# Byte addresses of SBUF tiles modulo 128, and three ones-products on TensorE, in a two-layer decoder trunk

## Chip, cores and metric

One NeuronCore of one Trainium2 chip. The metric is the device time of one execution in microseconds (us); lower is better.

## What is computed

Two layers of a decoder trunk on 256 tokens of width 1024, in float32. Each layer normalises the rows of x, scales and shifts them by a conditioning vector, mixes tokens with 8 stick-breaking and 8 sparse-attention heads, and then applies a channel mixer: a SwiGLU network of width 2816 in layer 0, the two best of eight experts of width 3584 in layer 1. Cut to what matters here:

```python
for layer in range(2):
    mod = silu(c) @ w_ada[layer] + b_ada[layer]        # six vectors of 1024
    h = rms_norm(x, g_pre_mix) * (1 + scale_m) + shift_m
    proj = h @ w_in                                    # q, k, v of all heads, gates
    merged = concat(rms_norm(o_sb, g_sb), rms_norm(o_nsa, g_nsa))
    x = x + gate_m * rms_norm(merged @ w_out, g_post_mix)
    h = rms_norm(x, g_pre_ffn) * (1 + scale_f) + shift_f
    f = swiglu(h) if layer == 0 else moe(h)            # router: h @ w_router + b_router, top 2 of 8
    x = x + gate_f * rms_norm(f, g_post_ffn)
```

## The kernel before

The work goes through five stages: layer 0's mixer (with a start that brings in x and the first weights), the dense channel mixer (`ffn`), layer 1's mixer, then routing and the eight experts (`moe`). Weights stream in by DMA, 1 MB a transfer, from the SP queue into the tiles `raw` (a ring of six) and, in the experts, also `unit`.

**Products.** Most of the matrix work runs in split form. A weight half-tile of 128x1024 is split by ScalarE (`whi`, L179) and VectorE (`wlo`, L180) into two parts of type float32r, the rows likewise (`hh` and `hlo` by `norm_parts` and `first`, `on` and `os` in the mixers, `gh`/`gl` and `xgh`/`xgl`/`g` in the channel mixers), and `mm3` (L193 to L197) makes three matmuls of them. A matmul has a stationary operand (128 columns, loaded ahead of it) and a moving operand that is streamed past. In two shapes the moving operand has:

- **256 columns**: the input projections and `ffn_gate`/`ffn_up`. Mostly `hh` or `hlo` moves past `whi`/`wlo` (`proj_t`, `ffn`); in `proj` (v of each head) the weights move past `hh`/`hlo`. `ffn` has 11 units of 96 such matmuls, each mixer some 530.
- **512 columns**: the output projection `wo`, `ffn_down` (into `acc`) and the large experts. The weights move past `on`/`os`, `gh`/`gl`, `xgh`/`xgl` or `g`. There are 96 in each `wo`, 264 in `ffn_down`, and 4 large experts with 504 each.

Four of the experts are small (64 slots): they use plain float32 and `unit`/`raw` themselves move (L1041).

**Addresses.** A tile pool puts tiles one behind another. The tile `sm` (L92) has 248 floats, or 992 bytes, `brow` (L122) 32 bytes, so that everything behind them starts off a multiple of 128 bytes. In the built program the start addresses modulo 128 are, with what each is used as in `mm3`:

| tiles | layer 0's mixer | ffn | layer 1's mixer | experts |
|---|---|---|---|---|
| `raw`, `unit`, `whi`, `wlo` | 64 | 64 | 64 | 64 |
| `hh`, `hlo` | 0 | 64 | 64 | |
| `on`, `os` | 0 | | 64 | |
| `gh`, `gl`; `xgh`, `xgl`, `g` | | 64 | | 64 |

So a 256-column matmul has its two operands at remainders 0 and 64 in layer 0 and at 64 and 64 in `ffn` and layer 1; a 512-column one 64 and 0 in layer 0's `wo`, and 64 and 64 everywhere else.

**Three small products with ones.** The squares of the mixers' outputs are summed over channels on TensorE: `sparse` (L706 to L709) multiplies the four 128x128 quarters of `sq` by a column of ones, in each of two row blocks t; `stick` (L758 to L763) keeps four tiles `sqs`, one for each pair of heads, and does eight such products at its end. `level` (L826 to L836) multiplies eight columns of the shift with eight slices of the router's weights and adds the bias. Each float32 matmul here shows as two instructions in the profile.

**Order.** A scheduler places the instructions of each engine by estimated times; an engine then runs its own list strictly in order.

Of the kernel before, what the change touches and what calls it, by code (L numbers as in the profile page):

```python
# [15 lines left out]
OP = mybir.AluOpType  # L16
AX = mybir.AxisListType
# [43 lines left out]
class Kernel:  # L61
# [28 lines left out]
    def setup(self, st):  # L90
        tc, nc, const = self.tc, self.nc, self.const
        self.sm = const.tile([P, SM_N], F32, name="sm")  # L92
        nc.sync.dma_start(self.sm, self.ins["sm"])
        self.sc = self.mix.tile([P, SC_N], F32, name="sc")
# [26 lines left out]
        nc.vector.tensor_scalar(self.tie, self.tie, 0.0, None, op0=OP.is_lt)  # L121
        self.brow = const.tile([P, E], F32, name="brow")  # L122
        nc.sync.dma_start(self.brow, self.ins["moe_b"].to_broadcast([P, E]))
# [171 lines left out]
    def norm_parts(self, l, ph, gain, scale_i, shift_i):  # L295

        nc = self.nc
        ss, sh = self.affine(l, gain, scale_i), self.mod(l, shift_i)
        xn = self.rows(ph)
        hh, hl = (ph.tile([P, KT, S], F32R, name=n, tag="h8") for n in ("hh", "hlo"))  # L300
        for t in range(2):
            for h in range(2):
                p = self.bank("ps"[h], "xnT").rearrange("p (k t) -> p k t", k=4)
                hf = ph.tile([P, 4, P], F32, name="hf", tag="t2")
                for i in range(4):
                    k = 4 * h + i
# [11 lines left out]
        return hh, hl  # L318

    def first(self, ph):  # L320


        nc = self.nc
        oh = ph.tile([33, W], F32, name="oh", tag="t2")
        nc.sync.dma_start(oh, self.ins["onehot"])
        tab = ph.tile([33, 8], F32, name="tab")
        nc.vector.memset(tab, BIG)
# [7 lines left out]
        xn = self.rows(ph)  # L335
        hh, hl = (ph.tile([P, KT, S], F32R, name=n, tag="h8") for n in ("hh", "hlo"))
        banks = [self.bank("ssoopp"[i], "first").rearrange("p (m t) -> p m t", m=2) for i in range(6)]
# [10 lines left out]
        for q in range(4):  # L348
# [65 lines left out]
    def mixer(self, l, ph):  # L414
        nc = self.nc
# [83 lines left out]
        kcT, vc = self.compress(l, ph, cb)  # L499
        on = ph.tile([P, 2, 4, S], F32R, name="on", tag="h8")  # L500
        ssn = self.sparse(l, ph, qn, ks, vs, kcT, vc, gt, on)
# [42 lines left out]

        os_ = ph.tile([P, 2, 4, S], F32R, name="os", tag="h8")
        pairs = self.stick(l, ph, qT, kT, vv, os_)
        next(pairs)
        next(pairs)
        if l:
            level = self.level(l)  # L550
        wout(1, on, ssn, first)
# [54 lines left out]
    def sparse(self, l, ph, qn, ks, vs, kcT, vc, gt, out):  # L606


        nc = self.nc
        ssn = ph.tile([P, 2], F32, name="ssn")  # L610
        for t in range(2):
# [213 lines left out]

    def level(self, l):  # L826
# [40 lines left out]
    def route(self, ph, gt, eq):  # L867
# [551 lines left out]
```

## Time and profile before

| | |
|---|---|
| median of 3 runs | 1452.79 us (1452.57 to 1456.24) |
| the profiled execution | 1452.78 us, span of its instructions 1451.0 us |
| TensorE busy | 1379.9 us, 95% of the span, 7470 matmuls |
| VectorE, ScalarE busy | 977.9 us (67%), 770.0 us (53%) |
| HBM read | 479.87 MB, 332 GB/s over the span |

A matmul's busy time in this profile includes the way through the array, so that matmuls overlap and a busy TensorE is not TensorE at its peak. The pace of a run of matmuls is read from their start times: last start less first start, over the number of steps between them.

### The profile page before, as it was taken

Reading aid. Unit: us, or ns where it says so; the run is one execution under the profiler, and the core shown is the slowest. Engines: PE = TensorE matmul, PEld = TensorE weight load, DVE = VectorE, ACT = ScalarE, POOL = GpSimd, SP = SyncE. Lnnn points to the kernel's source line nnn. Section 1 sums busy time; section 2 is a strip of 40 time slices with the busy share of each in tenths; the row PEclk is TensorE's granted clock in tenths of the full one; section 3 lists DMA queues with packets and bytes.
Section 4 is the critical chain, followed back from the end, with each engine's and each line's share of the span. In section 5 each row is a group of like instructions: output and inputs, shape, how many; then the busy total and the mean of one; then the engine's idle time right before and its main releaser. Section 6 shows DMA issues by size and latency. Waiting matters only on the chain.

```text
span 1451.0 us, 20370 instructions
## 1 busy us (share of the span) xinstructions
PE 1379.9 (95%) x7470; PEld 988.8 (68%) x7470; DVE 977.9 (67%) x1566; ACT 770.0 (53%) x1179; POOL 16.5 (1%) x24
## 2 busy tenths in 40 slices
PE   5899969999979999999999999999999999999996
PEld 5767759999877687544788534887435888788432
DVE  7678888877565774522999424998315989999413
ACT  3464654444554556232787324787324778787322
POOL 0100010000100000000000000000000000000000
PEclk9989979999979999799999999999999999999998
DMA  9936829888435284899999999999999999999994
GB/s 365 326 143 210 337 82 344 316 309 315 176 119 203 88 319 132 353 400 420 419 421 420 419 419 420 420 420 421 418 421 420 420 420 407 345 368 375 369 421 182
DMA packets 73479, 482.52 MB, mean 333 GB/s; under 512 B 10315, under 2 KB 10484, under 8 KB 18588
## 3 DMA queue, kind: packets, MB, share of 16 engines
q1 hardware_dynamic: 72876, 479.91, 83.7%
q0 software_dynamic: 496, 1.25, 0.4%
q8 instruction: 60, 0.98, 0.3%
q14 instruction: 47, 0.39, 0.1%
HBM read 479.87 MB, written 1.25 MB: 332 GB/s over the span
## 4 chain that ended last, share of the span: by engine, by line
PE 64%; DVE 3%; ACT 1%; issue 1%; DVEq 0%; ACTq 0%
PE moe_gate L1041 7%; PE moe_up L1041 7%; PE yacc L1041 7%; PE moe_gate L196 4%; PE moe_gate L195 4%; PE moe_gate L197 4%; PE yacc L196 3%; PE yacc L195 3%; PE yacc L197 3%; PE moe_up L196 3%; PE moe_up L197 3%; PE moe_up L195 3%; PE gT L1099 2%; PE gather L1177 1%; DVE wlo L180 1%; PE po L618 1%
## 5 line engine op out<-in xcount | busy, mean ns | idle before, releaser
L179 ACT ACTIVATE whi<-raw 128x1024 fp32r<-128x1024 f32 x260 | 271.7, 1058 | 162.6 <-PE ffn_gate L196 33.0
L180 DVE TENSOR_TENSOR wlo<-raw,whi 128x1024 fp32r<-128x1024 f32 x256 | 307.0, 1223 | 74.1 <-ACT whi L179 68.8
L180 DVE TENSOR_TENSOR wlo<-unit,whi 128x1024 fp32r<-128x1024 f32 x202 | 236.7, 1221 | 9.3 <-ACT whi L179 5.4
L179 ACT ACTIVATE whi<-unit 128x1024 fp32r<-128x1024 f32 x202 | 208.4, 1057 | 34.0 <-PE moe_up L197 16.1
L207 DVE CUSTOM_DVE_ANT_0 raw<-raw,cb,sm 128x1024 f32<-128x1024 f32 x96 | 120.7, 1279 | 3.1 <-DMA raw<-in_w_ada_dram 3.1
L1089 DVE TENSOR_TENSOR sg<-moe_gate,sg 64x512 f32<-64x512 f32 x28 | 19.1, 681 | 113.5 <-ACT sg L1088 113.5
L196 PE MATMUL moe_up<-wlo,xgh 128*128 128x512 f32 x224 | 88.6, 395 | 3.9 <-DVE wlo L180 3.9
L196 PE MATMUL yacc<-wlo,g 128*128 128x512 f32 x224 | 89.3, 399 | 0.3 <-DVE wlo L180 0.3
L195 PE MATMUL moe_gate<-whi,xgh 128*128 128x512 f32 x224 | 88.2, 394 | 0.0
L195 PE MATMUL yacc<-whi,g 128*128 128x512 f32 x224 | 88.0, 393 | 0.0
L196 PE MATMUL moe_gate<-wlo,xgh 128*128 128x512 f32 x224 | 87.9, 392 | 0.0
L195 PE MATMUL moe_up<-whi,xgh 128*128 128x512 f32 x224 | 87.7, 392 | 0.0
L197 PE MATMUL yacc<-whi,g 128*128 128x512 f32 x224 | 87.4, 390 | 0.0
L197 PE MATMUL moe_up<-whi,xgl 128*128 128x512 f32 x224 | 87.4, 390 | 0.0
L197 PE MATMUL moe_gate<-whi,xgl 128*128 128x512 f32 x224 | 87.4, 390 | 0.0
L1089 DVE TENSOR_TENSOR up<-moe_up,up 64x512 f32<-64x512 f32 x28 | 19.1, 683 | 72.7 <-ACT up L1088 72.7
L1041 PE MATMUL moe_up<-unit,xf 128*64 128x512 f32 x288 | 66.3, 596 | 0.0
L1041 PE MATMUL yacc<-unit,gf 128*64 128x512 f32 x272 | 62.2, 593 | 0.0
L1041 PE MATMUL moe_gate<-unit,xf 128*64 128x512 f32 x240 | 57.1, 598 | 0.0
L1088 ACT ACTIVATE sg<-moe_gate 64x512 f32<-64x512 f32 x28 | 16.6, 594 | 72.6 <-PE moe_gate L1041 72.6
L195 PE MATMUL ffn_gate<-hh,whi 128*128 128x256 f32 x176 | 51.2, 291 | 2.5 <-ACT hh L315 2.4
L196 PEld LDWEIGHTS moe_up<-wlo,xgh 128*128 128x128 f32 x224 | 42.0, 188 | 16.6 <-DVE wlo L180 8.2
(410 smaller groups left out, 2926.1 us busy)
## 6 DMA issues: line engine op xcount, KB each, us to landing
unit<-in_moe_gate_dram SPq DMA_DIRECT2D x66, 1024.0 KB, 14.9
unit<-in_moe_up_dram SPq DMA_DIRECT2D x56, 1024.0 KB, 14.6
unit<-in_moe_down_dram SPq DMA_DIRECT2D x54, 1024.0 KB, 16.1
raw<-in_w_ada_dram SPq DMA_DIRECT2D x48, 1024.0 KB, 6.5
raw<-in_moe_gate_dram SPq DMA_DIRECT2D x46, 1024.0 KB, 14.5
raw<-in_moe_down_dram SPq DMA_DIRECT2D x45, 1024.0 KB, 15.6
raw<-in_moe_up_dram SPq DMA_DIRECT2D x44, 1024.0 KB, 13.7
raw<-in_w_in_dram SPq DMA_DIRECT2D x16, 1024.0 KB, 5.8
```

The source lines that it names most:

```text
L179: self.last_hi = nc.scalar.activation(hi, w, AF.Copy)
L180: last_lo = (nc.gpsimd if self.count < 2 else nc.vector).tensor_sub(lo, w, hi.bitcast(F32))
L195: nc.tensor.matmul(out, lhsT=ahi, rhs=bhi, start=first, stop=False, skip_group_check=True)
L196: nc.tensor.matmul(out, lhsT=ahi, rhs=blo, start=False, stop=False, skip_group_check=True)
L197: nc.tensor.matmul(out, lhsT=alo, rhs=bhi, start=False, stop=last, skip_group_check=True)
L207: self.nc.vector.tensor_tensor_reduce(w[:, j], w[:, j], self.cb, 1.0, self.sm[:, b:b + 1], OP.mult, OP.add, self.modc[:, l, o:o + 1])
L618: nc.tensor.matmul(po[64 * g:64 * g + 64, :], lhsT=lhs, rhs=rhs, start=first[g], stop=last, skip_group_check=True)
L1041: m = nc.tensor.matmul(out[64 * kk:64 * kk + 64], lhsT=x[:, k], rhs=w[:, 512 * kk:512 * kk + 512], start=first and h == 0, stop=last and h ...
L1088: nc.scalar.activation(to, p[64:128], AF.Copy)
L1089: nc.vector.tensor_add(to, p[0:64], to)
L1099: nc.tensor.transpose(tr[0][:, j, 0:n], sg[0:n, P * j:P * j + P], self.ident[0:n, 0:n])
L1177: nc.tensor.matmul(p[:, a], lhsT=self.x[:, t, P * k:P * k + P], rhs=both[:, t], start=a == 0 and t == 0, stop=t == 1, skip_group_check=True)
```

## The change

1. `sm` and `brow` get some unused columns at their ends, and so do `tab`, `ssn`, `sss` and `selb`, so that tiles of 128 bytes or more start at multiples of 128 bytes. `raw`, `unit`, `whi`, `wlo`, `gh`, `gl`, `xgh`, `xgl`, `g` are then at remainder 0 in every stage.
2. `hh` and `hlo` come from a tile with 128 bytes more, of which they use the part that starts 64 bytes in (`off`): remainder 64 in every stage. `on` and `os` use the start of such a tile (`split_of`): remainder 0.
3. `sparse` sums the four quarters of `sq` on VectorE into `sqz` (128x128), then makes one product instead of four. `stick` adds the squares of pairs 1 to 3 to those of pair 0 on VectorE (`sqsum`), then makes two products instead of eight. `level` multiplies and sums on VectorE (`each`, `both`) and makes one product with the tile of minus ones.

The operands of `mm3` then have these remainders (moving, stationary): 256 columns 64 and 0 where `hh`/`hlo` move, 0 and 64 in `proj`; 512 columns 0 and 0 everywhere.

```diff
+LINE = 32
-        self.sm = const.tile([P, SM_N], F32, name="sm")
-        nc.sync.dma_start(self.sm, self.ins["sm"])
+        self.sm = const.tile([P, -(-SM_N // LINE) * LINE], F32, name="sm")
+        nc.sync.dma_start(self.sm[:, 0:SM_N], self.ins["sm"])
-        self.brow = const.tile([P, E], F32, name="brow")
+        self.brow = const.tile([P, 2 * E], F32, name="brow")[:, 0:E]
...
-        hh, hl = (ph.tile([P, KT, S], F32R, name=n, tag="h8") for n in ("hh", "hlo"))
+        hh, hl = (self.off(ph, n) for n in ("hh", "hlo"))
...
+    def off(self, ph, name):
+
+        t = ph.tile([P, KT * S + LINE], F32R, name=name, tag="h8")
+        return t[:, LINE // 2:LINE // 2 + KT * S].rearrange("p (k t) -> p k t", k=KT)
+
+    def split_of(self, ph, name):
+        t = ph.tile([P, KT * S + LINE], F32R, name=name, tag="h8")
+        return t[:, 0:KT * S].rearrange("p (a k t) -> p a k t", a=2, k=4)
...
-        on = ph.tile([P, 2, 4, S], F32R, name="on", tag="h8")
+        on = self.split_of(ph, "on")
...
+            sqz = ph.tile([P, P], F32, name="sqz", tag="t2")
+            nc.vector.tensor_reduce(sqz, sq.rearrange("p (z t) -> p t z", z=4), axis=AX.X, op=OP.add)
             pr = self.bank("t", "ssn")
-            for z in range(4):
-                nc.tensor.matmul(pr[:, 0:1], lhsT=sq[:, P * z:P * z + P], rhs=self.ones, start=z == 0, stop=z == 3)
+            nc.tensor.matmul(pr[:, 0:1], lhsT=sqz, rhs=self.ones, start=True, stop=True)
...
-            sq = ph.tile([P, S], F32, name="sqs", bufs=4)
+            sq = ph.tile([P, S], F32, name="sqs", bufs=2) if pr else sqs
             nc.scalar.activation(sq, po[:, 0:S], AF.Square)
-            sqs.append(sq)
+            if pr:
+                nc.vector.tensor_add(sqs, sqs, sq)
...
-            for pr in range(4):
-                nc.tensor.matmul(prs[:, t:t + 1], lhsT=sqs[pr][:, P * t:P * t + P], rhs=self.ones, start=pr == 0, stop=pr == 3)
+            nc.tensor.matmul(prs[:, t:t + 1], lhsT=sqs[:, P * t:P * t + P], rhs=self.ones, start=True, stop=True)
...
-        sh = self.mod(l, 3)
+        each = ph.tile([P, KT, E], F32, name="each")
+        nc.vector.tensor_tensor(each, wr, self.mod(l, 3)[:, :, None].to_broadcast([P, KT, E]), op=OP.mult)
+        both = ph.tile([P, LINE], F32, name="both")[:, 0:E]
+        nc.vector.tensor_reduce(both, each.rearrange("p k e -> p e k"), axis=AX.X, op=OP.add)
         pc = self.bank("t", "level")
-        for k in range(KT):
-            nc.tensor.matmul(pc[:, 0:E], lhsT=sh[:, k:k + 1].to_broadcast([P, P]), rhs=wr[:, k], start=k == 0, stop=k == KT - 1)
+        nc.tensor.matmul(pc[:, 0:E], lhsT=self.negone, rhs=both, start=True, stop=True)
         level = self.small.tile([P, E], F32, name="level")
-        nc.vector.tensor_tensor(level, pc[:, 0:E], self.brow, op=OP.add)
+        nc.vector.scalar_tensor_tensor(level, pc[:, 0:E], -1.0, self.brow, op0=OP.mult, op1=OP.add)
```

How the lists of the engines change, at three places of layer 1's mixer. Line numbers of the changed kernel are some ten higher from `off` on.

TensorE where `level` stands, in the second pair of heads of `stick` (`z` and `sbo` are its logits and outputs, `wo` the output projection), before:

```order
L739 MATMUL z<-sbe,negone 128x128
L740 MATMUL z<-sbe,negtri 128x128
L746 MATMUL sbo<-sbe,vv 64x256
L833 MATMUL level<-sm,modc 128x8 x6
L746 MATMUL sbo<-sbe,vv 64x256
L749 MATMUL sbo<-sbe,vv 64x128 x2
L833 MATMUL level<-sm,modc 128x8 x2
L196 MATMUL wo<-wlo,on 128x512
```

and now:

```order
L751 MATMUL z<-sbe,negtri 128x128
L757 MATMUL sbo<-sbe,vv 64x256
L846 MATMUL level<-both,negone 128x8
L197 MATMUL wo<-wlo,on 128x512
L757 MATMUL sbo<-sbe,vv 64x256
L760 MATMUL sbo<-sbe,vv 64x128 x2
L198 MATMUL wo<-whi,on 128x512
```

The eight products of `level` have become one, ahead of the same `sbo`.

VectorE after the second row block of `sparse` (`on` is its split output, `ISA raw,modc` the sums for the conditioning vector), before:

```order
L704 SCALAR_TENSOR_TENSOR on<-po,sm,on 128x128
L709 COPY ssn<-ssn 128x1
L207 ISA raw,modc<-raw,cb,sm 128x1024
L207 ISA modc 128x1
L704 SCALAR_TENSOR_TENSOR on<-po,sm,on 128x128
L226 TENSOR_SCALAR rov<-ssn,halfeps 128x2
L180 TENSOR_TENSOR wlo<-raw,whi 128x1024
L704 SCALAR_TENSOR_TENSOR on<-po,sm,on 128x128
```

and now:

```order
L714 SCALAR_TENSOR_TENSOR on<-po,sm,on 128x128
L717 TENSOR_REDUCE sqz<-sq 128x128
L208 ISA raw,modc<-raw,cb,sm 128x1024
L208 ISA modc 128x1
L714 SCALAR_TENSOR_TENSOR on<-po,sm,on 128x128
L720 COPY ssn<-ssn 128x1
L181 TENSOR_TENSOR wlo<-raw,whi 128x1024
L714 SCALAR_TENSOR_TENSOR on<-po,sm,on 128x128
L227 TENSOR_SCALAR rov<-ssn,halfeps 128x2
L181 TENSOR_TENSOR wlo<-raw,whi 128x1024
```

The reduction into `sqz` stands behind the first `on`, two others of `on` behind it, and the copy of the sums waits for the one product that needs it.

TensorE at the end of `stick` (`rows` spreads a vector over all partitions), before:

```order
L746 MATMUL sbo<-sbe,vv 64x256
L761 MATMUL ssb<-ones,sqs 128x1 x3
L387 MATMUL rows<-ident,gc 128x128
L746 MATMUL sbo<-sbe,vv 64x256
L749 MATMUL sbo<-sbe,vv 64x128 x2
L387 MATMUL rows<-ident,gc 128x128 x4
L761 MATMUL ssb<-ones,sqs 128x1 x5
L387 MATMUL rows<-ident,gc 128x128 x3
L195 MATMUL wo<-whi,os 128x512
```

and now:

```order
L757 MATMUL sbo<-sbe,vv 64x256
L397 MATMUL rows<-ident,gc 128x128 x2
L757 MATMUL sbo<-sbe,vv 64x256
L760 MATMUL sbo<-sbe,vv 64x128 x2
L397 MATMUL rows<-ident,gc 128x128 x6
L196 MATMUL wo<-whi,os 128x512
L772 MATMUL ssb<-ones,sqsum 128x1 x2
L197 MATMUL wo<-wlo,os 128x512
```

The eight products `ssb` stood ahead of the first `wo`; the two that are left stand behind it.

## Rows read from the trace of the kernel before

**Rows 1.** The page: the chain that ended last, share of the span by engine.

```profile
PE 64%; DVE 3%; ACT 1%; issue 1%; DVEq 0%; ACTq 0%
```

**Rows 2.** Stages: us, busy PE, PEld, DVE, ACT, POOL, then PEclk, DMA share, GB/s.

```profile
75.00:205.00 130.00, 117.08 (x704) 87.35 (x704) 104.58 (x280) 77.74 (x195) 4.70 (x2) 0.92 0.53 194
205.00:395.00 190.00, 189.32 (x1321) 178.18 (x1322) 143.85 (x183) 87.67 (x102) 0.99 (x1) 0.98 0.78 288
395.00:590.00 195.00, 180.04 (x1181) 145.83 (x1180) 124.16 (x339) 103.02 (x247) 4.70 (x4) 0.91 0.47 169
590.00:1451.00 861.00, 838.60 (x3836) 528.82 (x3835) 552.59 (x649) 471.50 (x584) 0.00 (x0) 0.99 0.98 399
```

**Rows 3.** TensorE's timeline, one unit of `ffn`: first and last of 96 matmuls (start, duration).

```profile
236.97 0.28 PE L195 MATMUL ffn_gate<-hh,whi 128*128 128x256 f32 x1
...
248.37 0.28 PE L197 MATMUL ffn_up<-hh,wlo 128*128 128x256 f32 x1
```

**Rows 4.** The same, layer 0: first and last of 67, of 27 and of 58 matmuls.

```profile
31.86 0.28 PE L196 MATMUL first<-hlo,whi 128*128 128x256 f32 x1
...
39.54 0.28 PE L197 MATMUL first<-hh,wlo 128*128 128x256 f32 x1
...
116.51 0.28 PE L196 MATMUL pk<-hlo,whi 128*128 128x256 f32 x1
...
119.46 0.28 PE L195 MATMUL pk<-hh,whi 128*128 128x256 f32 x1
...
137.77 0.28 PE L440 MATMUL pv<-whi,hlo 128*128 128x256 f32 x1
...
144.49 0.28 PE L440 MATMUL pv<-whi,hlo 128*128 128x256 f32 x1
```

**Rows 5.** The same, `wo` of `os`: layer 0, first and last of 40; layer 1, of 39.

```profile
180.77 0.39 PE L196 MATMUL wo<-wlo,os 128*128 128x512 f32 x1
...
189.87 0.40 PE L197 MATMUL wo<-whi,os 128*128 128x512 f32 x1
...
568.10 0.39 PE L196 MATMUL wo<-wlo,os 128*128 128x512 f32 x1
...
576.75 0.39 PE L197 MATMUL wo<-whi,os 128*128 128x512 f32 x1
```

**Rows 6.** The same, a large expert: first and last of 71 matmuls.

```profile
731.37 0.39 PE L197 MATMUL yacc<-whi,g 128*128 128x512 f32 x1
...
747.28 0.39 PE L195 MATMUL yacc<-whi,g 128*128 128x512 f32 x1
```

**Rows 7.** The chain in order of time, a small expert: 16 matmuls of 512 columns.

```profile
614.42 3.43 PE yacc L1041 x16
```

**Rows 8.** Groups by line: engine, operation, tiles, shape, count, busy, mean ns, idle.

```profile
L195 PE MATMUL moe_gate<-whi,xgh 128*128 128x512 f32 x224 | 88.2, 394 | 0.0
L195 PE MATMUL ffn_gate<-hh,whi 128*128 128x256 f32 x176 | 51.2, 291 | 2.5 <-ACT hh L315 2.4
```

**Rows 9.** The chain in order of time, layer 1's mixer (start, us, engine, tile, line).

```profile
478.15 1.05 PE ssn L708 x8
...
526.73 1.14 DVE wlo L180
...
541.60 1.44 PE level L833 x12
...
543.83 0.54 PE level L833 x4
...
564.18 0.76 PE ssb L761 x6
...
566.48 1.17 PE ssb L761 x10
```

**Rows 10.** Groups by line and shape on VectorE: count, busy us, mean ns.

```profile
L936 DVE TENSOR_REDUCE ranked<-cgt 128x16 f32<-128x128 f32 x4 | 1.1, 278 | 0.0
...
L481 DVE TENSOR_TENSOR gs<-gr,gs 128x256 fp32r<-128x256 f32 x2 | 0.9, 426 | 0.0
```

More of the change, by code (lines that the diff above doesn't have):

```diff
@@ L325, in first @@
         nc.sync.dma_start(oh, self.ins["onehot"])
-        tab = ph.tile([33, 8], F32, name="tab")
+        tab = ph.tile([33, LINE - 8], F32, name="tab")[:, 0:8]
         nc.vector.memset(tab, BIG)
@@ L335, in first @@
         xn = self.rows(ph)
-        hh, hl = (ph.tile([P, KT, S], F32R, name=n, tag="h8") for n in ("hh", "hlo"))
+        hh, hl = (self.off(ph, n) for n in ("hh", "hlo"))
         banks = [self.bank("ssoopp"[i], "first").rearrange("p (m t) -> p m t", m=2) for i in range(6)]
@@ L543, in second @@
                     score(1, (last.ins,))
-        os_ = ph.tile([P, 2, 4, S], F32R, name="os", tag="h8")
+        os_ = self.split_of(ph, "os")
         pairs = self.stick(l, ph, qT, kT, vv, os_)
@@ L549, in mixer @@
         if l:
-            level = self.level(l)
+            level = self.level(l, ph)
         wout(1, on, ssn, first)
@@ L609, in sparse @@
         nc = self.nc
-        ssn = ph.tile([P, 2], F32, name="ssn")
+        ssn = ph.tile([P, LINE], F32, name="ssn")[:, 0:2]
         for t in range(2):
@@ L715, in stick @@
         rs = [slice(0, 64), slice(64, 128)]
-        sqs = []
+        sqs = ph.tile([P, S], F32, name="sqsum")
         for pr in range(4):
@@ L759, in stick @@
         for t in range(2):
-            for pr in range(4):
-                nc.tensor.matmul(prs[:, t:t + 1], lhsT=sqs[pr][:, P * t:P * t + P], rhs=self.ones, start=pr == 0, stop=pr == 3)
-        sss = ph.tile([P, 2], F32, name="sss")
+            nc.tensor.matmul(prs[:, t:t + 1], lhsT=sqs[:, P * t:P * t + P], rhs=self.ones, start=True, stop=True)
+        sss = ph.tile([P, LINE], F32, name="sss")[:, 0:2]
         nc.vector.tensor_copy(sss, prs[:, 0:2])
@@ L823, in ffn, with level @@
             self.update(ph, t, lambda n: None if n is None else acc[t][n], gm, nc.vector)
-    def level(self, l):
+    def level(self, l, ph):
         nc = self.nc
         wr = self.sm[:, SM_WR:SM_WR + 64].rearrange("p (k e) -> p k e", k=8)
-        sh = self.mod(l, 3)
+        each = ph.tile([P, KT, E], F32, name="each")
+        nc.vector.tensor_tensor(each, wr, self.mod(l, 3)[:, :, None].to_broadcast([P, KT, E]), op=OP.mult)
+        both = ph.tile([P, LINE], F32, name="both")[:, 0:E]
+        nc.vector.tensor_reduce(both, each.rearrange("p k e -> p e k"), axis=AX.X, op=OP.add)
         pc = self.bank("t", "level")
-        for k in range(KT):
-            nc.tensor.matmul(pc[:, 0:E], lhsT=sh[:, k:k + 1].to_broadcast([P, P]), rhs=wr[:, k], start=k == 0, stop=k == KT - 1)
+        nc.tensor.matmul(pc[:, 0:E], lhsT=self.negone, rhs=both, start=True, stop=True)
         level = self.small.tile([P, E], F32, name="level")
-        nc.vector.tensor_tensor(level, pc[:, 0:E], self.brow, op=OP.add)
+        nc.vector.scalar_tensor_tensor(level, pc[:, 0:E], -1.0, self.brow, op0=OP.mult, op1=OP.add)
         return level
@@ L884, in route @@
         nc.vector.tensor_reduce(sel, gt, axis=AX.X, op=OP.add)
-        selb = ph.tile([P, 2 * E], BF16, name="selb")
+        selb = ph.tile([P, LINE], BF16, name="selb")[:, 0:2 * E]
         nc.vector.tensor_scalar(selb, sel.rearrange("p t e -> p (t e)"), 2.0, None, op0=OP.is_lt)
```

## The prediction

> **What bounds the kernel now.** I read the page's chain first: of the span, 64% is TensorE and 3% VectorE [rows 1] (the rest of the share could not be followed back, so the stages were read one by one). Then busy time by stage [rows 2]. In `ffn` TensorE is busy for 189.32 of 190 us with DMA at 0.78, so a matmul that goes faster there shortens the stage by as much. In the experts it is busy for 838.6 of 861 us while DMA moves 399 GB/s at a share of 0.98: TensorE sets the end, with DMA close behind. In the two mixers TensorE shows 117 of 130 and 180 of 195 us, but much of that is latency of short dependent steps, and VectorE has 104.6 of 130 and 124.2 of 195; there a saving counts only where TensorE's list is what the next step waits for. The granted clock is 0.91 to 0.99 in the mean, so nearly all work runs at the upper level, 2.4 GHz; nothing in the change makes TensorE pause longer, and I leave the clock out.
>
> A busy time includes the way through the array, so the pace of a run of matmuls has to be taken from start times. In `ffn`, 96 matmuls of 256 columns start from 236.97 to 248.37: 11.40 us over 95 steps, **120.0 ns** each [rows 3]. The same shape in layer 0 shows other paces [rows 4]: 7.68 us over 66 steps is 116.4 ns, 2.95 over 26 is 113.5, 6.72 over 57 is 117.9. With 512 columns, `wo` goes the other way [rows 5]: layer 0 9.10 us over 39 steps, **233.3 ns**; layer 1 8.65 over 38, **227.6 ns**. A large expert has 15.91 us over 70, 227.3 ns [rows 6]. Instructions, shapes and clock are the same; what differs by layer is where the tiles start. With 256 columns the faster runs have operands at different remainders (0 and 64, whichever of the two moves), the slower ones at 64 and 64. With 512 columns different remainders are the slower.
>
> **The change, part by part.**
>
> *256 columns in `ffn`.* They go from 64 and 64 to 64 and 0, the kind that layer 0 has. There are six groups of 176, 1,056 in all [rows 8]; the stage's granted clock of 0.98 [rows 2] is 190 x 0.02 / 0.5 = 7.6 us at the lower level, at 213 ns each some 36 matmuls, which gain nothing. That leaves 1,020 x (120.0 - 116.4) = **3.7 us**. The ends are 117.9 (2.1 us) and 113.5 (6.6 us) [rows 4]; I take 116.4 because it is the longest run of the three and lies between two paces that each hold on for dozens of matmuls, so that both must be expected. No cover: the stage is TensorE's.
>
> *256 columns in layer 1.* The first four projections (240 matmuls, some 210 at full clock) run alone at the stage's start: 210 x 3.6 = **0.8 us** (0.4 to 1.4). The 288 for q, k and v fill gaps between steps of the sparse heads, and while the last of them run the chain is VectorE's (a `wlo` of 1.14 us at 526.73 [rows 9]); zero, and 1.0 us if that cover were gone. In layer 0 both operands only swap remainders: zero.
>
> *512 columns.* In layer 0's `wo`, 96 matmuls go from different to equal remainders: 96 x (233.3 - 227.6) = **0.5 us**. The 264 of `ffn_down`, the 2,016 of the large experts (nine groups of 224 like the one in [rows 8]) and layer 1's `wo` go from 64 and 64 to 0 and 0. No run of before has that in this shape. From below, 512 columns pass in 3.43/16 = 214 ns in the small experts [rows 7]; from above stands the 233.3 of [rows 5]. For 2,280 matmuls these are 30 us gained and 13.7 us lost. I take 227.3, no change: equal remainders before and after are nearest to the rows with equal remainders, and with 256 columns it made no difference which of the two operands was at 64. Both ends are kept below.
>
> *The products with ones.* In layer 1's chain `ssn` takes 1.05 us in the first row block, `level` 1.44 + 0.54, `ssb` 0.76 + 1.17 [rows 9]: 8, 16 and 16 instructions of some 0.12 us. Two, two and four are left.
> - `level`: 1.98 - 0.25 = 1.7 us. Its two operations on VectorE, some 0.2 us each, stand in the norm at the head of layer 1's mixer, where VectorE pauses for ScalarE; 0.2 us of them are counted as exposed. Net **1.5 us**.
> - `ssb`: 1.93 - 0.45 = 1.5 us. Of the three additions of 128x256, 0.43 us each by the same size at 426 ns [rows 10], the last stands between the last square and the product; net **1.0 us**. The product now waits behind the first `wo`, and all of TensorE's list behind it waits with it; `os` of the last pair, which `wo` needs anyway, comes at the same time.
> - `ssn`: 0.8 us in the first row block. The reduction of 512 elements is not in the trace; 128 elements cost 278 ns [rows 10], so by 256 elements at 426 it is some 0.72 us. In the first block other work on TensorE runs meanwhile; in the second VectorE is the chain and the 0.72 eats what TensorE saves. Net **0.8 us**, between a loss of 0.6 and a gain of 1.6.
> - In layer 0 the same without `level`, with VectorE busier (0.80 of the stage): taken at somewhat over half of 1.8, **1.0 us**, between nothing and 1.8.
>
> Sum: 3.7 + 0.8 + 0.5 + 1.5 + 1.0 + 0.8 + 1.0 = 9.3 us. All of it lies ahead of the experts, whose weights begin to stream when the mixers' tiles come free, so the whole last stage moves forward with it, loads and products alike. The profiled execution took 1452.78 us, 1.8 above its span and equal to the median of 1452.79. Forecast: 1452.8 - 9.3 = **1443.5 us**. A measurement of this kernel tells 0.3%, 4.4 us, from no change.
>
> A rule that speaks against this: the Trainium skill, TensorE: Matmul & The Clock Gate, Back-to-back issue gap, gives the pace by the columns alone, N/2.4 + 2.5 ns, that is 109.2 ns at 256 and 215.7 at 512, with no address in it; and its section Step-by-step: what each phase is for has the moving operand and the next weights on two independent read ports, so that one takes nothing from the other. By that rule the moved tiles are worth nothing and the sum is 4.3 us. The trace does not agree: one shape has 113.5, 116.4, 117.9 and 120.0 ns [rows 3, 4], none of them 109.2.
>
> **The rivals.**
>
> *Multiples of 128 also quicken the 512-column matmuls.* If a start at 0 on both sides saves there what the best run saves at 256 (120.0 - 113.5 = 6.5 ns), 2,280 x 6.5 = 14.8 us more: 1428.7. For it: 227.3 is 13 ns over the pace of [rows 7], so there is room. Against it: the swap symmetry above; and DMA, at a share of 0.98 already [rows 2], would have to move some 2% faster to follow.
>
> *Multiples of 128 slow them.* The 512-column matmuls at 0 and 0 run as layer 0's `wo`, 233.3 ns. 2,280 x 6.0 = 13.7 us lost in `ffn_down` and the experts, `wo` not gained: 1443.5 + 0.5 + 13.7 = 1457.7, slower. It decides from 9.3/2,280 = 4.1 ns on, a pace over 231.4. For it: the only 512-column run of before with an operand at 0 is the slow one. Against it: that operand stands against one at 64.
>
> *The address is not the cause.* Layers 0 and 1 could differ by what ScalarE and VectorE do beside the matmuls. Then only the products count: 1452.8 - 4.3 = 1448.5. Against it: `ffn` holds 120.0 through 95 steps [rows 3], and a mixed neighbourhood would scatter; for it, layer 0 itself has two paces.
>
> *VectorE takes back what TensorE saves.* Two reductions and three additions a layer are 2 x 0.72 + 3 x 0.43 = 2.7 us, 5.8 with `level` over both layers; where all of it lands on the chain, and the scheduler's other order of the sparse heads adds waits, the 4.3 us are gone and 5.0 are left: 1447.8.
>
> **How the numbers follow.** The forecast as summed has 0.52; quicker large matmuls 0.16; address without effect 0.12; VectorE 0.10; slower large matmuls 0.10. The range is 1426 to 1454: it reaches down to the first rival with its room, up past the third and the fourth and to both failing together (1452.8); outside are the slower rival and the far end of 30 us. The forecast's own range, with the bounds of its terms, is 1439 to 1448. Faster by over 0.3% (below 1448.4): the forecast nearly whole, the first rival, most of the fourth and a little of the third, 0.74. Within: 0.16, from the third and the tails. Slower: 0.10.
>
> **What would show it.** In the new profile the start times of `ffn_gate` and `ffn_up` should lie 113 to 118 ns apart, not 120; a unit of 96 should take 10.8 to 11.3 us instead of 11.4. `wo` of layer 0 should have 227, the large experts 227 as before. `level`, `ssn` and `ssb` should be gone from the chain but for a few tenths of a us. It is wrong if `ffn` keeps 120 ns, if the experts' stage changes its length by more than 3 us, or if the mixers grow although their products shrank.

## The result, and the profile after

The changed kernel takes 1441.2 us in the median of 5 runs (1440.77 to 1444.67), the kernel before beside it 1452.79 (1452.57 to 1456.24): a ratio of 0.992, 95% interval 0.9904 to 0.9937, or 11.6 us less. The forecast was 1443.5. The profiled execution took 1441.2 us, its span is 1439.4.

Where the time went is read by stage. The bounds are the last start of a `first` matmul, the first of `ffn_gate`, the last of `acc`, the first of `moe_gate` and the last of `scatter`. The windows of before (columns as in [rows 2]):

```profile
0.00:63.63 63.63, 44.30 (x313) 41.20 (x314) 49.35 (x104) 26.43 (x45) 6.14 (x18) 0.92 0.98 338
63.63:205.38 141.75, 127.60 (x823) 94.78 (x821) 108.33 (x295) 81.71 (x204) 4.70 (x2) 0.93 0.57 210
205.38:396.52 191.14, 190.84 (x1327) 179.44 (x1328) 144.99 (x182) 88.41 (x102) 2.51 (x1) 0.98 0.78 286
396.52:598.25 201.73, 185.84 (x1210) 151.72 (x1208) 125.31 (x352) 102.76 (x246) 3.18 (x4) 0.90 0.49 180
598.25:1437.72 839.47, 830.88 (x3801) 521.68 (x3800) 542.74 (x616) 467.86 (x572) 0.00 (x0) 1.00 0.99 404
```

and of the changed kernel:

```profile
0.00:61.34 61.34, 43.44 (x314) 40.31 (x314) 48.83 (x103) 26.35 (x45) 6.17 (x18) 0.92 0.97 346
61.34:204.82 143.48, 126.81 (x800) 93.47 (x798) 112.00 (x302) 81.31 (x204) 4.72 (x2) 0.92 0.55 210
204.82:392.94 188.12, 187.81 (x1327) 176.30 (x1328) 145.09 (x182) 88.34 (x102) 2.52 (x1) 0.99 0.78 291
392.94:586.89 193.95, 177.44 (x1172) 142.48 (x1171) 128.57 (x359) 102.72 (x246) 3.18 (x4) 0.92 0.51 187
586.89:1426.49 839.60, 831.00 (x3801) 521.92 (x3800) 542.92 (x616) 467.90 (x572) 0.00 (x0) 1.00 0.98 404
```

The start is 2.3 us shorter, layer 0 is 1.7 **longer**, `ffn` 3.0 shorter, layer 1 with the routing 7.8 shorter, the experts are the same: 11.2 us. Layer 0's VectorE is busy 3.7 us longer, and layer 1 has a granted clock of 0.92 instead of 0.90: (1 - 0.92) x 193.95 / 0.5 = 31 us at the lower level against 40.

TensorE's timeline of the changed kernel: a unit of `ffn` (first and last of 96 matmuls), `wo` of `os` in layer 0 (of 39), a large expert (of 71).

```profile
235.75 0.28 PE L196 MATMUL ffn_gate<-hh,whi 128*128 128x256 f32 x1
...
246.87 0.28 PE L198 MATMUL ffn_up<-hh,wlo 128*128 128x256 f32 x1
...
180.44 0.39 PE L198 MATMUL wo<-whi,os 128*128 128x512 f32 x1
...
189.26 0.39 PE L198 MATMUL wo<-whi,os 128*128 128x512 f32 x1
...
719.99 0.40 PE L198 MATMUL yacc<-whi,g 128*128 128x512 f32 x1
...
735.91 0.39 PE L196 MATMUL yacc<-whi,g 128*128 128x512 f32 x1
```

The unit now takes 11.12 us over 95 steps, 117.0 ns where it had 120.0 [rows 3]. `wo` takes 8.82 over 38, 232 ns, hardly less than the 233.3 of [rows 5]: there the forecast of 227 failed. The expert has 15.92 over 70, 227.4 ns, as before [rows 6].

The chain of layer 1's mixer, in order of time, now has:

```profile
474.28 0.97 DVE sqz L717
475.38 0.35 PE ssn L719 x2
...
513.53 0.33 PE ssn L719 x2
...
534.45 0.32 PE level L846 x2
...
556.93 0.38 ACT sqs L763
...
570.06 1.95 PE logits L875 x16
```

`level` has gone from 1.98 us to 0.32, `ssb` from 1.93 to nothing, with a square (`sqs`, 0.38) in its place [rows 9]. The reduction costs 0.97 us, not the estimated 0.72, and with the 0.35 of its product the step of `ssn` in the first row block has grown from 1.05 to 1.32 us. And the router's first `logits` take 1.95 us where before they took

```profile
579.86 3.37 PE logits L862 x16
```

although the change does not touch them: the same 16 instructions at another granted clock (its last fall begins at 580 us before, with the `logits`, and at 572 now, behind them).

### The profile page after: what moved, and what is told of

Same layout as the page of the kernel before. It is cut to its first block, busy times and chain, and to the rows that moved or that the text cites. A ratio compares the mean times of both kernels' runs of the same rounds, so it can differ in the third digit from the quotient of the medians.

```text
span 1439.4 us, 20261 instructions
## 1 busy us (share of the span) xinstructions
PE 1366.9 (95%) x7408; PEld 974.5 (68%) x7408; DVE 984.6 (68%) x1578; ACT 769.4 (53%) x1179; POOL 16.6 (1%) x24
## 4 chain that ended last, share of the span: by engine, by line
PE 65%; DVE 3%; ACT 1%; issue 1%; DVEq 0%; ACTq 0%
PE moe_gate L1054 7%; PE moe_up L1054 7%; PE yacc L1054 7%; PE moe_gate L197 4%; PE moe_gate L196 4%; PE moe_gate L198 4%; PE yacc L197 4%; PE yacc L198 3%; PE yacc L196 3%; PE moe_up L197 3%; PE moe_up L198 3%; PE moe_up L196 3%; PE gT L1112 2%; PE gather L1190 1%; PE po L628 1%; DVE wlo L181 1%
## 5 line engine op out<-in xcount | busy, mean ns | idle before, releaser
L1102 DVE TENSOR_TENSOR sg<-moe_gate,sg 64x512 f32<-64x512 f32 x28 | 19.1, 681 | 113.4 <-ACT sg L1101 113.4
```

The costliest lines, as they stand in the source:

```text
L1102: nc.vector.tensor_add(to, p[0:64], to)
```

## The experiments

The theory (A): the pace of a matmul depends on whether its two operands start alike (at the same remainder), and the products with ones save what each of them cost on the chain. Rivals: the new order of the work, not the address (B); the modulus (C); starts off a multiple of 128 as such (D); one of the three products alone, through the order of the sparse heads (F), against each product for itself (E). The start addresses are those of the built programs; the traces do not show them.

Times and stage lengths are read apart. Times on the later chips spread by several us, and they go with the granted clock that each execution lists: over 141 executions, a line for each kernel with one common slope gives 0.81 us for each 0.001 of the mean clock (95% 0.65 to 0.97). The last column of the first table is that line at a clock of 0.972, with its 95% interval; "at equal clock" below means this column. It takes the clock as given: what a change does to the clock itself is left out of it. Stage lengths are free of it where the time at the lower level is equal: `ffn` has 190.3, 190.3 and 190.1 us in ones_only, d0 and ssn1, all with alike operands. d128 and x512 ran once, 1443.3 and 1447.7 us.

| kernel | median us | ratio to before, 95% | at clock 0.972 |
|---|---|---|---|
| before | 1452.8 | | 1451.5 ± 0.6 |
| changed | 1441.2 | 0.992 (0.9904 to 0.9937) | 1443.0 ± 1.8 |
| addr_only | 1448.4 | 0.997 (0.9953 to 0.9987) | 1447.5 ± 1.2 |
| ones_only | 1446.5 | 0.9953 (0.9938 to 0.9968) | 1448.5 ± 1.7 |
| d0 | 1446.6 | 0.9955 (0.9939 to 0.997) | 1448.6 ± 1.7 |
| d192 | 1439.7 | 0.9903 (0.9887 to 0.992) | 1441.3 ± 1.8 |
| d64 | 1442.6 | 0.9924 (0.9901 to 0.9947) | 1443.5 ± 1.8 |
| ssn1 | 1452.0 | 0.9992 (0.9976 to 1.0009) | 1452.3 ± 1.2 |
| ssb1 | 1448.5 | 0.9974 (0.9955 to 0.9992) | 1449.1 ± 1.2 |
| lv1 | 1451.3 | 0.9997 (0.9977 to 1.0016) | 1450.5 ± 1.3 |
| ssn_l1 | 1440.0 | 0.9909 (0.9884 to 0.9934) | 1440.4 ± 1.6 |
| ssn_undone | 1442.3 | 0.9936 (0.9916 to 0.9955) | 1442.5 ± 1.6 |

Stage lengths of the profiled executions, by the bounds given above, and the time at the lower clock level in the two mixers, added up from the granted clock (its records are 0.5 or 1.0). Each row is one execution:

| us | start | layer 0 | ffn | layer 1 | experts | lower level, layer 0 and 1 |
|---|---|---|---|---|---|---|
| before | 63.6 | 141.8 | 191.1 | 201.7 | 839.5 | 21.2, 42.0 |
| changed | 61.3 | 143.5 | 188.1 | 194.0 | 839.6 | 21.9, 31.9 |
| addr_only | 60.9 | 141.0 | 188.5 | 200.8 | 839.9 | 17.8, 38.4 |
| ones_only | 60.9 | 142.8 | 190.3 | 194.7 | 840.8 | 17.1, 32.5 |
| d192 | 66.4 | 142.4 | 187.1 | 193.1 | 840.4 | 18.9, 30.5 |
| d0 | 61.0 | 142.8 | 190.3 | 194.7 | 839.8 | 17.1, 32.0 |
| d128 | 60.7 | 143.4 | 190.4 | 194.1 | 839.9 | 20.5, 31.7 |
| d64 | 63.0 | 143.1 | 188.2 | 193.4 | 839.6 | 20.5, 32.1 |
| ssn1 | 63.1 | 144.0 | 190.1 | 200.1 | 839.7 | 20.5, 38.1 |
| ssb1 | 63.6 | 140.9 | 191.4 | 196.2 | 840.8 | 20.6, 29.4 |
| lv1 | 63.3 | 141.9 | 191.1 | 199.3 | 840.6 | 21.4, 39.6 |
| ssn_l1 | 63.0 | 142.3 | 187.0 | 193.4 | 840.1 | 25.8, 30.8 |
| ssn_undone | 62.8 | 141.7 | 187.9 | 195.0 | 839.9 | 23.9, 31.4 |
| x512 | 61.1 | 143.2 | 188.1 | 193.4 | 847.2 | 20.5, 31.9 |

### The two halves of the change

**addr_only**, from the changed kernel:

```diff
-            nc.vector.tensor_reduce(sqz, sq.rearrange("p (z t) -> p t z", z=4), axis=AX.X, op=OP.add)
-            nc.tensor.matmul(pr[:, 0:1], lhsT=sqz, rhs=self.ones, start=True, stop=True)
+            for z in range(4):
+                nc.tensor.matmul(pr[:, 0:1], lhsT=sq[:, P * z:P * z + P], rhs=self.ones, start=z == 0, stop=z == 3)
...
```

with `stick` and `level` put back likewise.

> The changed kernel's tile addresses with the products with ones as they were before. Theory A (the pace of a matmul follows from the difference of its two operands' start addresses): ffn as in the changed kernel, 117.0 ns a matmul of 256 columns and some 3 us shorter than before; layer 1's first projections 0.6 us shorter; time 1446 to 1449 us, that is 4 to 7 above the changed kernel's 1441.2. Rival B (the address is not the cause, the other order of work is): ffn keeps 120.0 ns and the time is 1452 to 1453.

**ones_only**, from the kernel before: the hunks of `sparse`, `stick` and `level` as in the change, without the padding; one line of each is shown.

```diff
+            nc.vector.tensor_reduce(sqz, sq.rearrange("p (z t) -> p t z", z=4), axis=AX.X, op=OP.add)
...
+                nc.vector.tensor_add(sqs, sqs, sq)
...
+        nc.tensor.matmul(pc[:, 0:E], lhsT=self.negone, rhs=both, start=True, stop=True)
```

> The kernel before, with its addresses, and only the three products with ones moved to VectorE. Theory A: ffn keeps 120.0 ns; both mixers gain what the products cost: 0.6 us in layer 0, 4 to 7 in layer 1; time 1445 to 1448. Rival B: ffn at 117.0 and the time near 1441.

TensorE's timeline, one unit of `ffn` in addr_only,

```profile
249.84 0.28 PE L196 MATMUL ffn_gate<-hh,whi 128*128 128x256 f32 x1
...
260.96 0.28 PE L198 MATMUL ffn_up<-hh,wlo 128*128 128x256 f32 x1
```

and in ones_only:

```profile
251.40 0.28 PE L196 MATMUL ffn_gate<-hh,whi 128*128 128x256 f32 x1
...
262.79 0.28 PE L198 MATMUL ffn_up<-hh,wlo 128*128 128x256 f32 x1
```

11.12 and 11.39 us over 95 steps: 117.0 and 119.9 ns. The pace goes with the addresses and not with the products, as A expects; B falls. At equal clock the addresses are worth 4.0 us (± 1.3), the products 3.0 (± 1.8); the prediction had 5.0 and 4.3.

### Which addresses

**d192**, **d0**, **d128** and **d64** set the remainder modulo 256 of moving minus stationary address (where `hh`/`hlo` move) to one value in every stage, and have `on`/`os` at 0. From the changed kernel (48, 0, 32 or 16 floats for `hh` and `hlo`; `l0` makes up for layer 0's tiles standing 128 bytes on):

```diff
-        t = ph.tile([P, KT * S + LINE], F32R, name=name, tag="h8")
-        return t[:, LINE // 2:LINE // 2 + KT * S].rearrange("p (k t) -> p k t", k=KT)
+        t = ph.tile([P, KT * S + 2 * LINE], F32R, name=name, tag="h8")
+        o = self.at(name)
+        return t[:, o:o + KT * S].rearrange("p (k t) -> p k t", k=KT)
...
+    def at(self, name):
+        return {'hh': 48, 'hlo': 48, 'on': 0, 'os': 0}[name] + self.l0 & 63
...
+        self.l0 = 0 if l else LINE
```

> The changed kernel with each of hh and hlo placed so that moving minus stationary address is 192 modulo 256 in every stage (where hh moves), and on and os at 0 modulo 256. Theory A with modulus 256: 256 columns at 113.3 to 114.5 ns in ffn instead of 117.0, some 3 us less there; layer 0's wo of os at 227 instead of 232, layer 1's wo of on at 227 instead of 229 to 238; in all 1436 to 1439 us. Rival C (only the remainder modulo 128 counts, 64 here as in the changed kernel): ffn stays at 117, time 1441 within 1 us.

> The changed kernel with hh, hlo, on and os all at the remainder of whi and wlo modulo 256. Theory A: 120.0 ns for 256 columns in every stage, layer 0 too, so ffn 3 us longer than in the changed kernel and layer 0 and 1 each 0.5 to 1.5 longer, wo at 227 in both layers (1 us gained): 1443 to 1446. Rival D (what slows 256 columns before is that both operands start off a multiple of 128, not that they start alike): ffn at 113 to 118 ns, time 1438 to 1441.

> The changed kernel with hh and hlo 128 bytes off whi and wlo modulo 256, and on and os at 0. Theory A with modulus 128 for 256 columns: 120.0 ns in every stage, as where the two start alike. Theory A with modulus 256: one of the paces of unlike starts, 113.4 to 117.8 ns, in ffn and both mixers. ffn (first ffn_gate to the end of acc) 190.3 us by the first, 186 to 188.5 by the second.

> d192 with hh and hlo at 64 instead of 192 modulo 256; wo stays at 0 and 0. Theory G (only alike or unlike modulo 128 counts, and each run of matmuls then holds one of two paces): 256 columns at 113.4 or 117.8 ns in ffn, never 120; ffn 186.5 to 188.5 us, time 1439 to 1442. Rival H (64 and 192 are two different cases, and the 113.4 of d192 belongs to 192): ffn at 117.0 to 117.8 throughout, 188.1 to 188.8 us. Should all ten later units hold 113.4, ffn would be some 184.

TensorE's timeline of d192: the first 172 matmuls of `ffn` at full clock, the next unit, and `wo` of `os` in layer 0 (39).

```profile
213.80 0.28 PE L198 MATMUL ffn_gate<-hh,wlo 128*128 128x256 f32 x1
...
233.18 0.28 PE L198 MATMUL ffn_up<-hh,wlo 128*128 128x256 f32 x1
...
238.75 0.28 PE L196 MATMUL ffn_gate<-hh,whi 128*128 128x256 f32 x1
...
249.94 0.28 PE L198 MATMUL ffn_up<-hh,wlo 128*128 128x256 f32 x1
...
184.48 0.40 PE L198 MATMUL wo<-whi,os 128*128 128x512 f32 x1
...
193.13 0.39 PE L198 MATMUL wo<-whi,os 128*128 128x512 f32 x1
```

19.38 us over 171 steps is 113.3 ns; 11.19 over 95 is 117.8, **at the same addresses**. The fifth unit has 113.4 again (89 matmuls), the others 117.8. `wo` has 8.65 over 38, 227.6 ns.

d0, 67 matmuls of `first` in layer 0 and a unit of `ffn`:

```profile
42.32 0.28 PE L197 MATMUL first<-hlo,whi 128*128 128x256 f32 x1
...
50.23 0.28 PE L198 MATMUL first<-hh,wlo 128*128 128x256 f32 x1
...
251.55 0.28 PE L196 MATMUL ffn_gate<-hh,whi 128*128 128x256 f32 x1
...
262.94 0.28 PE L198 MATMUL ffn_up<-hh,wlo 128*128 128x256 f32 x1
```

119.8 and 119.9 ns: layer 0, which had 113 to 118 before, in the changed kernel and in d192, slows to 120 as soon as its operands start alike, at multiples of 128 and of 256. D falls. At equal clock d0 and ones_only are 0.2 us apart (± 2.3): with operands alike no gain of the moved addresses is seen.

The same two places in d128:

```profile
42.09 0.28 PE L197 MATMUL first<-hlo,whi 128*128 128x256 f32 x1
...
49.93 0.28 PE L198 MATMUL first<-hh,wlo 128*128 128x256 f32 x1
...
251.87 0.28 PE L196 MATMUL ffn_gate<-hh,whi 128*128 128x256 f32 x1
...
263.26 0.28 PE L198 MATMUL ffn_up<-hh,wlo 128*128 128x256 f32 x1
```

118.8 and 119.9: nearly the pace of alike, with a second value beside it. d64 has 117.8 in all units of `ffn` (188.2 us) and 113.3 over 18 steps of `pq`. What decides between 113.4 and 117.8 at one address stays open: d192 shows both, and the changed kernel, with `hh` at 64 and `hlo` at 192 in `ffn`, 117.0. For d64 H's figures in `ffn` were met (117.8 and 188.2 us), but its rule fails at `pq`, which has 113.3 at 64.

d192 is 1.0 us shorter in `ffn` than the changed kernel, where 3 were expected, and its 1439.7 us are above the 1436 to 1439 expected. So at 256 columns C does not fall: 64 and 192, one case modulo 128, share the paces 113 to 118, and 0 and 128, the other, have 118 to 120. It is `wo`, with 512 columns, that tells 128 from 0. Why the pace follows the two addresses at all is not shown by any run.

**x512** asks whether the large experts depend on it at all, and on which remainder. From the changed kernel:

```diff
-            gh = ph.tile([P, 2, S], F32R, name="gh", bufs=2)
-            gl = ph.tile([P, 2, S], F32R, name="gl", bufs=2)
+            gh, gl = (ph.tile([P, 2 * S + 2 * LINE], F32R, name=n, bufs=2) for n in ("gh", "gl"))
+            gh, gl = (g[:, 48:48 + 2 * S].rearrange("p (k t) -> p k t", k=2) for g in (gh, gl))
...
+    def rows_at(self, ph, name):
+        o = 16 if name == "xgh" else 0
+        return ph.tile([P, KT * P + 16], F32R, name=name, tag="x4")[:, o:o + KT * P].rearrange("p (k t) -> p k t", k=KT)
```

> The changed kernel with xgh and xgl 64 bytes further (512 columns of moe_gate and moe_up then start at 0 and 64 modulo 256), gh and gl 192 further (ffn_down 0 and 192), and g left where it is (yacc at 0 and 0). Theory A: moe_gate, moe_up and ffn_down at 231 to 234 ns, yacc at 227.3; 1,344 matmuls of the large experts cost 5 to 9 us, so the stage from the first moe_gate to the last scatter takes 845 to 849 us instead of 839.6, and ffn some 1.3 us more. Rival: only wo, in the mixers' neighbourhood, has 232, and the experts stay at 227.3 and 839.6.

Its timeline, first and last of 71 matmuls of a large expert:

```profile
702.35 0.40 PE L198 MATMUL yacc<-whi,g 128*128 128x512 f32 x1
...
718.61 0.39 PE L196 MATMUL yacc<-whi,g 128*128 128x512 f32 x1
```

16.26 us over 70, 232.3 ns against 227.4; 48 of the 71 are of `moe_gate` and `moe_up`. Split by tile, the step after a matmul of `moe_gate` or `moe_up` is 233.3 ns in the mean (227.6 in the changed kernel), after one of `yacc`, whose operands were left alike, 229.5 (228.4). 1,344 x 5.7 = 7.7 us; the stage is 7.6 longer, as A expects. `ffn_down` runs at 229.8 in a unit's 24 matmuls (228.3 in the changed kernel), less than the 231 to 234 expected: that part missed. That `ffn` did not grow says little, since it has 3.4 us at the lower level here and 5.4 in the changed kernel, worth up to 1.0 us.

So the sign turns with the width: at 256 columns alike is slow (119.9) and unlike quick, at 512 alike is quick (227) and unlike slow (230 to 233); and 128 bytes apart counts as nearly alike at 256, as unlike at 512 (`wo` of `os` in layer 0, 232).

### The three products one by one

**ssn1**, **ssb1** and **lv1** are the kernel before with one part each, of which a line is shown.

```diff
+            nc.vector.tensor_reduce(sqz, sq.rearrange("p (z t) -> p t z", z=4), axis=AX.X, op=OP.add)
```

```diff
+            if pr:
+                nc.vector.tensor_add(sqs, sqs, sq)
```

```diff
+        nc.tensor.matmul(pc[:, 0:E], lhsT=self.negone, rhs=both, start=True, stop=True)
```

> The kernel before with the change of sparse alone (sqz, one product for each row block). Each mixer is measured from the end of its first projections, or of ffn, to the start of what follows. Theory E (each product gives its own term): layer 1 is 0.8 us shorter, 1.6 at most; layer 0 is 1.0 us longer, as in the run with all three products, because the reduction of 0.97 us stands in its chain. Rival F (the 7 us that the three products gave layer 1 come from one of them, through a new order of the sparse heads): layer 1 is 4 us shorter or more here. Time near 1453 by E, near 1449 by F.

> The kernel before with the change of stick alone (sqsum, two products for eight). Theory E: layer 1 1.0 to 1.9 us shorter, layer 0 shorter by 0 to 0.8; time 1451 to 1452.5. Rival F: layer 1 shorter by 4 us or more, time 1449 or less.

> The kernel before with the change of level alone. Theory E: layer 1 1.5 to 2.0 us shorter, layer 0 and ffn as before; time 1451 to 1452. If a further 1.3 us go in the logits of the router, which took 3.37 us before and 2.09 with all three products, the raised clock there comes with level; 3.0 to 3.4 us in layer 1 in all.

In layer 1 they gave 1.6, 5.5 and 2.5 us: 9.6, more than the 7.0 of all three. ssb1's 5.5 and its 1448.5 us miss what E expected and meet F's bounds, but over half of it lies ahead of the first sum of squares in `stick`, where its lists in layer 1 do not differ from before: 13 us of the sparse heads are at a granted clock of 0.87 before,

```profile
465.00:478.00 13.00, 13.00 (x68) 8.10 (x68) 6.87 (x31) 5.89 (x16) 0.00 (x0) 0.87 0.16 53
```

and in ssb1 at 1.00, with 81 matmuls for 68:

```profile
465.00:478.00 13.00, 12.95 (x81) 8.25 (x80) 8.35 (x39) 8.92 (x27) 0.00 (x0) 1.00 0.24 81
```

ssb1 has 12.6 us less at the lower level in layer 1, at half speed up to 6.3 us. What is left for the edit can be read from the chain, in ssb1

```profile
537.93 1.44 PE level L833 x12
...
574.87 2.21 PE logits L862 x16
```

and in lv1:

```profile
541.38 0.32 PE level L836 x2
...
578.21 2.23 PE logits L865 x16
```

Counted from the start of layer 1, `level` begins at 145.1 us before [rows 9] and at 142.1 in ssb1: 3.0 of the 5.5 us are won before anything differs in this layer. The first `logits` give 1.2 more (3.37 to 2.21), by the clock; 1.3 us are left for the change of `stick`.

In lv1 `level` begins at 145.2, and of the 2.5 us 1.1 are the `logits`: 1.3 are left for the change of `level`, where 1.5 to 2.0 were expected. That the raised clock in the `logits` comes with `level` is not borne out, since ssb1 has it too. ssn1's 1.6 us go with 3.9 us less at the lower level, worth up to 1.9: for the change of `sparse` nothing is shown to be left in layer 1.

So F's new order is not what did it. At equal clock the three times differ from before by +0.8, -2.4 and -1.0 us, each ± 1.4; together -2.6 ± 2.7, beside ones_only's -3.0. E fits better than F, with smaller terms than it had.

The clock itself differs between these kernels. In the traces, one execution each, the ten kernels with the change of `stick` have 29 to 33 us at the lower level in layer 1, the four without it 38 to 42. Over all executions the mean granted clock is 0.9705 before (60 executions), 0.9706 in addr_only, 0.9699 in lv1 and 0.9723 in ssn1; with the change of `stick` it is 0.9718 to 0.9748. But ssb1 alone has 0.9723, no more than ssn1, which leaves `stick` as it was: which part raises the clock, and how, is not shown. By the slope, the changed kernel's 0.9730 is worth 2.0 us over 0.9705.

In layer 0 the clock does not cover it: ssn1 is 2.3 us **longer** there, at nearly the same time at the lower level (20.5 and 21.2). VectorE's timeline, in the first row block, shows how. Before,

```profile
102.32 0.35 DVE L704 SCALAR_TENSOR_TENSOR on<-po,sm,on 128x128 fp32r<-128x128 f32 x1
103.08 0.16 DVE L709 COPY ssn<-ssn 128x1 f32<-128x1 f32 x1 [0.42 <-PE ssn L708]
103.16 0.16 DVE L625 TENSOR_TENSOR smx<-smx,gt 128x8 f32<-128x8 f32 x1
```

and in ssn1:

```profile
101.82 0.35 DVE L704 SCALAR_TENSOR_TENSOR on<-po,sm,on 128x128 fp32r<-128x128 f32 x1
102.09 1.04 DVE L707 TENSOR_REDUCE sqz<-sq 128x128 f32<-128x512 f32 x1
103.05 0.16 DVE L625 TENSOR_TENSOR smx<-smx,gt 128x8 f32<-128x8 f32 x1
...
103.67 0.16 DVE L710 COPY ssn<-ssn 128x1 f32<-128x1 f32 x1 [0.20 <-PE ssn L709]
```

From `on` to the copy of the sums it was 0.76 us and is 1.85; `smx`, on which the next heads' weights rest, stands behind the reduction. Counted from the start of the stage, the copy comes 1.1 us later in the first row block and 2.6 in the second. In this run four products of TensorE cost layer 0 less than one reduction.

**ssn_l1** and **ssn_undone**, from d192: `sparse` as before in layer 0 only, or in both.

```diff
...
+            if l:
+                sqz = ph.tile([P, P], F32, name="sqz", tag="t2")
+                nc.vector.tensor_reduce(sqz, sq.rearrange("p (z t) -> p t z", z=4), axis=AX.X, op=OP.add)
+                nc.tensor.matmul(pr[:, 0:1], lhsT=sqz, rhs=self.ones, start=True, stop=True)
+            else:
+                for z in range(4):
+                    nc.tensor.matmul(pr[:, 0:1], lhsT=sq[:, P * z:P * z + P], rhs=self.ones, start=z == 0, stop=z == 3)
```

> The run with 192 modulo 256 (d192), but in layer 0 sparse makes its four products with ones as before; layer 1 has the reduction. From the run with the change of sparse alone, layer 0 (end of the first projections to the first ffn_gate) should be 2.3 us shorter than d192's 142.4, some 140.1, and layer 1 as there, 193.1: 1437 to 1438 us. Rival: with the squares of stick on VectorE too, layer 0 is bound elsewhere and stays at 142.4: 1439.7.

> d192 with sparse as before in both layers; stick and level stay changed. If the three parts add up, layer 1 loses the 1.7 us that the change of sparse gave alone, 194.8, layer 0 gains 2.3: 1439 us. Rival: in layer 1 the reduction stands in the way of what the change of stick gave alone (5.5 us), and layer 1 is 191 to 193 here: 1435 to 1437.

ssn_l1 keeps layer 0 at 142.3, the rival's figure, but with 25.8 us at the lower level for d192's 18.9, so its trace decides nothing; at equal clock it is 0.9 ± 2.4 us under d192. ssn_undone's layer 1 is 195.0, as the sum of parts expects, and its layer 0 0.7 shorter where 2.3 were expected, again with more time at the lower level (23.9), worth up to 2.5 us; its 1442.3 us are above both figures expected. So that layer 0 is better off without the reduction rests on ssn1 and ones_only and was not gained back here. d192 and ssn_l1 have the lowest medians, 1.5 and 1.2 us under the changed kernel; at equal clock that is 1.7 ± 2.5 and 2.6 ± 2.4, and no more than a hint.

## Why the prediction was right

The total came within 2.3 us, in part by luck: layer 0 lost 1.7 us where the sum had 1.5 gained, layer 1 gained 7.8 where it had 4.1, and the start gave 2.3 that it did not have. The main term, the addresses in `ffn`, holds by its own pace.

- *256 columns in `ffn`*, 3.7 us: right in mechanism and nearly in size. The stage is 3.0 shorter, 2.7 by addresses alone (addr_only). 117.0 ns came where 116.4 was taken. That 116.4 is no third pace: in its run of 67 [rows 4] the first 44 steps take some 118 ns each, the last 22 some 113.5.
- *256 columns in layer 1*, 0.8: from the first `pc` matmul to the last `pgT` it went from 34.56 to 33.83 us, up to 0.4 of it by the clock; these projections run at 117.7 to 117.8 ns in the changed kernel, which for 210 matmuls is 0.4 us and not 0.8.
- *Layer 0's `wo`*, 0.5: **this step failed.** It counted remainders modulo 128, by which `os` and the weights start alike; modulo 256 they are 128 apart, and `wo` keeps 232 ns. With both at 0 modulo 256 it has 227.6 (d192) and 227.9 (d0). For `on` the gain came, 233.6 to 229.2 ns in the mean, but in layer 1 `on` went from 227.8 to 233.1, which the sum had as unchanged; over both layers nothing is left of the 0.5.
- *The experts unchanged*, 227.3 ns: right (227.4), by the symmetry taken from 256 columns. x512 shows what the choice was worth: 7.6 us in the experts alone.
- *`level`*, 1.5, and *`ssb`*, 1.0: the chain lost 1.66 and, less the square, 1.93 - 0.38 = 1.55 us. Each made alone and without the clock's part they are worth 1.3 and 1.3 us (above): right in kind, the first a little too large, the second a little too small.
- *`ssn`*, 0.8: **not borne out.** The reduction costs 0.97 us and not 0.72, by which the chain's step grew from 1.05 to 1.32 us; ssn1's 1.6 us in layer 1 can be the clock's, and in layer 0 the change of `sparse` is a loss.
- *Layer 0's products*, gain 1.0: **wrong sign.** 1.0 us lost in ones_only, 2.3 in ssn1. The rival in which VectorE takes back what TensorE saves holds in this stage; in layer 1 it holds for `ssn` at most.
- *"I leave the clock out"*: **mis-sized.** With addresses equal, the products shorten layer 1 by 6.8 us (addr_only to changed), where the sum had 3.3; 6.5 us less at the lower level account for up to 3.2 of the difference of 3.5. It is read in windows of the two traces: before,

```profile
495.00:500.00 5.00, 5.00 (x32) 5.00 (x32) 4.47 (x12) 1.55 (x2) 0.00 (x0) 0.68 0.54 187
```

and at the same place of the work in the changed kernel:

```profile
490.00:495.00 5.00, 5.00 (x43) 4.84 (x42) 5.00 (x16) 1.54 (x2) 0.00 (x0) 1.00 0.55 202
```

43 matmuls instead of 32 in 5 us. This one stretch does not go along with the change of `stick`: ssb1 has one at the lower level there too, 95 us into layer 1, and ssn1 has none. The prediction's ground, that nothing in the change makes TensorE pause longer, looked for a loss only.
- *The start*, not forecast: 2.3 us shorter, yet ones_only, with the addresses of before, has 60.9 too, and d192 66.4. It is not shown to be an effect of the change.
- *The rule set against the forecast*: the Trainium skill, TensorE: Matmul & The Clock Gate, Back-to-back issue gap, gives N/2.4 + 2.5 ns as the gap of an isolated matmul and lets weight load and matmul together set the spacing of a stream. The rows are streams, so 109.2 ns was not the figure to hold against them; they show 113.3 to 120.0 ns at one width, by address.

At equal clock the change gives 8.5 us (± 1.9); made alone, the addresses give 4.0 and the products 3.0. The forecast of 9.3 did not have the 2.0 that go with the clock.

## What to carry to other kernels

Read the pace of a matmul shape from start times in every stage, and compare the operands' start addresses modulo 256, not 128, before blaming anything else; then test with an offset, since the sign depends on the width. Moving a small product off TensorE paid here for `level` and `ssb`, and not for `ssn`, whose reduction stands in VectorE's way. And before crediting a stage's gain to an edit, set the granted clock of the stretch beside it.

## What was not expected of the hardware

- Two paces at one address and one shape: 113.3 and 117.8 ns in d192, each held for 88 to 171 steps. No run shows what chooses between them.
- Opposite signs: alike costs 119.9 against 113 to 118 at 256 columns, and saves 1.5 to 6 ns at 512.
- Loads got quicker. The profile page's rates in 40 slices, ones_only with `raw` and `unit` at 192 modulo 256, then the changed kernel with 0:

```profile
GB/s 367 337 137 204 339 99 349 308 309 318 177 122 203 88 321 176 383 384 419 420 420 420 420 416 420 420 419 421 419 419 420 420 419 403 348 370 375 371 421 183
```

```profile
GB/s 370 341 130 189 342 94 350 322 318 331 161 123 203 91 319 176 393 400 426 426 426 426 400 413 426 426 426 426 396 425 426 427 425 378 338 371 372 375 426 179
```

420 against 426 GB/s at saturation, and so in every run: 420 in ssn1, ssb1 and lv1, 426 in addr_only and all placings from the changed kernel. It goes with the addresses; that it is the remainder of `raw` and `unit` was not tried by itself. The experts' stage is no shorter for it (839.5 us before, 839.6 now). The Trainium skill, DMA: Bandwidth & Descriptors, How a descriptor splits into AXI transactions, has reads begin at multiples of 256 bytes and a start off them cost more; what moved here is the written side.
